# Residual tiles laid over the other branch half, late operand transposes on four banks, and the sample rows' gate and up products from the split weight pieces

## The chip, the cores and the metric

The kernel runs on one core of one Trainium2 chip. The metric is the device time of one execution in microseconds (us), lower is better. The cores' engines are called by these names: PE is TensorE, which multiplies matrices (PEld is its weight load, which stands on rows of its own), DVE is VectorE, ACT is ScalarE, POOL is GpSimd, and SP issues most of the DMA transfers.

## The reference, cut to what matters

One inference layer is computed for 1024 prompt rows and, with the same weights, for 64 sample rows (8 sequences of 8). The part that the change touches is the end of the mixing part and the convolutional feed-forward network (FFN):

```python
merged = ga * (o @ w_br_attn) + gb * (pool_out @ w_br_pool) + gm * (om @ w_br_mem)
x = x + merged @ w_out
...
h = rmsnorm(x, norm2_g)
g = h @ w_gate                       # 1024 x 2816
u = h @ w_up                         # 1024 x 2816
ext = concatenate([prefix, g])       # two rows of state ahead of each sequence
gc = conv_b + sum(conv_w[j] * ext[j:j + L] for j in range(3))
x = x + (gelu(gc) * u) @ w_down      # 2816 x 1024
```

## The kernel before, in words

All products are float32 in quality. An operand is split into a high part (a cast to the fast format, on ACT) and a low part (the difference, on DVE; helper `split`, L109 and L110), and three passes high-high, high-low and low-high are summed.

**Branch stage.** The gated branches are projected with operand tiles `ob[c][i]`, where c is the half of the tokens and i the high or low part. They live in a pool `p3`. When it closes, pool `p5` takes its place in SBUF: the residual tiles `x1_0` to `x1_7` (128 rows each), `x1s` (the 64 sample rows) and the gain `g2b` lie over the `ob` tiles, and each may be written only when the `ob` tile under it has been read for the last time.

**Output projection.** L187 multiplies by `w_out` into two PSUM banks called nat, L925 adds the residual, L926 sums squares, and L932 normalizes. SP issues in program order: the weights of `w_out` (L159), the first FFN weights (L911), `g2b` (L919), `x1s` (L948), and the eight residual tiles (L950).

**FFN operands.** The FFN's gate and up products use one level of the Strassen-Winograd scheme: seven products of quarter blocks in place of eight. The prompt's operands are B11, B21, B22 and T1 to T4; T1 to T4 are built from sums and differences (L981 to L984). `put` transposes one 128x512 piece with four PE transposes (L106) into a PSUM bank, and splits it from there. The banks of `put` come from `tpb()`, which hands out two banks, tp and av, in turn. T1 and T2 are put as soon as the tiles are normalized; T3 and T4 come last, in the loop over `late`: T3 of a pair of tiles, then T4.

**FFN products.** For each of 22 column blocks m (even m gate, odd m up; 256 columns each) `products(m)` issues seven products of 12 matmuls (L1108), each 128 weight columns by 512 wide: with weight pieces a11 (tile wA), s1 (wB), s2 (wB), a12 (wA), s3 (wC), s4 (wC), a22 (wD). Results are copied (ACT: L1127, L1130, L1133, L1145) and added (DVE: `acc`, L1124) into `gu` tiles. Between products the generator `prep(m + 1)` moves on by a step: it makes the split pieces of the next block. The convolution (L1015 to L1018) follows an even m, the product of gate and up on POOL (L1162) an odd one, and the result goes to memory (`f_d`).

**The sample rows.** `sample_ffn(m, raw)`, a generator in two halves, multiplies the 64 sample rows with the unsplit float32 weights (L1031): eight matmuls of 64 weight columns by 256 wide, which take 16 PE instructions. Its second half transposes the result (`gs`), convolves it (`conv_s`, L1022 to L1024) in an even m, and multiplies in an odd m into `fsv`. After m = 21, `fs` is the split of `fsv`.

**Down projection.** L1221 multiplies the prompt's `fh` (the split of `fr`, read back from `f_d`) with the split weights `wd`, and L1228 the sample's `fs` with the same weights.

Instructions run in order on each engine; their order across the program is decided by a scheduler when the program is built.

## Time and profile before

| | us |
|---|---|
| median of 3 runs | 1809.1 (1806.98 to 1810.25) |
| the profiled execution: its own time | 1810.49 |
| its span, first to last instruction | 1808.7 |
| PE busy in the span | 1739.5 (96%) |
| DVE, ACT, POOL busy | 899.2 (50%), 717.2 (40%), 391.7 (22%) |
| mean granted clock of TensorE | 0.987 |

A busy share close to 100% means that the engine sets the pace where that holds. Rows of a timeline give the start, the duration of the whole group, the engine, the line, the operation with its output and inputs, the shapes and the count; in brackets stands the engine's idle time before the group and what ended it. A granted clock of 1.00 is 2.4 GHz, and 0.50 is 1.2 GHz.

### The profile page before, as it was taken

To read this page: it belongs to the slowest core of one execution; us is meant where nothing else is said; L and a number is where in the kernel's file an instruction comes from. 1 tells how busy PE (TensorE), PEld (TensorE's weight loads), DVE (VectorE), ACT (ScalarE), POOL (GpSimd) and SP (SyncE) were. 2 spreads that over 40 slices of the span, in tenths; PEclk is the share of its full clock that TensorE was granted. 3 is DMA by queue.
4 is the path that set the end of the run, shared out by engine and by line. 5 is a ranking of instruction groups with operands and counts; after the bars stand their busy time and mean duration, and the time that the engine had idled before them with its cause. 6 is when DMAs were issued, how large, how long until landed. Compare 5 with 4: busy or idle time off the path is not lost.

```text
span 1808.7 us, 22927 instructions
## 1 busy us (share of the span) xinstructions
PE 1739.5 (96%) x8285; PEld 1334.1 (74%) x8285; DVE 899.2 (50%) x1543; ACT 717.2 (40%) x1396; POOL 391.7 (22%) x427
## 2 busy tenths in 40 slices
PE   7999999998999999999989899999999999999997
PEld 5887876764666777767767677777777777888876
DVE  6411134230221666677716676666666666336464
ACT  5321235331222666665413343333333334234343
POOL 1113020301101324112201344444444442000000
PEclk9999999999999999999989899999999999999999
DMA  7441251468565323154432222222222223646563
GB/s 276 139 142 66 83 183 38 135 187 266 195 230 178 96 79 117 56 193 161 145 122 88 49 72 71 71 71 71 71 71 71 71 71 135 226 145 217 197 229 109
DMA packets 137367, 234.74 MB, mean 130 GB/s; under 512 B 25679, under 2 KB 71533, under 8 KB 137253
## 3 DMA queue, kind: packets, MB, share of 16 engines
q1 hardware_dynamic: 122117, 187.16, 32.5%
q0 software_dynamic: 15136, 46.12, 6.8%
q8 instruction: 65, 1.06, 0.2%
q14 instruction: 49, 0.40, 0.1%
HBM read 182.74 MB, written 50.54 MB: 129 GB/s over the span
## 4 chain that ended last, share of the span: by engine, by line
PE 82%; issue 7%; DVE 4%; DMA 3%; ACT 2%; POOL 1%; SPq 1%; POOLq 0%; ACTq 0%; DVEq 0%
PE nat L178 17%; PE big L1108 17%; PE big L1221 10%; PE nat L1108 7%; PE nat L187 6%; PE big L178 4%; PE nat L1221 3%; PE tp L1031 3%; PE tp L106 3%; PE av L106 2%; PE av L804 2%; PE big L774 2%; PE nat L195 2%; PE av L542 1%; PE big L523 1%
## 5 line engine op out<-in xcount | busy, mean ns | idle before, releaser
L178 PE MATMUL nat<-act,hl 128*128 128x512 f32 x1344 | 357.7, 404 | 0.0
L178 PEld LDWEIGHTS nat<-act,hl 128*128 128x128 f32 x1344 | 242.1, 189 | 61.0 <-issue 14.0
L187 PE MATMUL nat<-hl,act 128*128 128x512 f32 x768 | 186.6, 401 | 10.1 <-ACT nat L926 8.3
L1221 PE MATMUL big<-wd,fh 128*128 128x512 f32 x792 | 187.4, 390 | 4.1 <-ACT big L1189 2.5
L187 PEld LDWEIGHTS nat<-hl,act 128*128 128x128 f32 x768 | 146.5, 193 | 42.3 <-ACT nat L926 8.7
L1221 PEld LDWEIGHTS big<-wd,fh 128*128 128x128 f32 x792 | 148.3, 188 | 36.3 <-ACT big L1189 3.4
L1108 PE MATMUL big<-B,wA 128*128 128x512 f32 x528 | 130.5, 395 | 0.1
L110 DVE TENSOR_TENSOR hl<-raw,hl 128x1024 fp32r<-128x1024 f32 x52 | 66.4, 1287 | 123.8 <-ACT hl L109 112.8
L110 DVE TENSOR_TENSOR wd<-wr,wd 128x1024 fp32r<-128x1024 f32 x66 | 84.5, 1282 | 74.1 <-ACT wd L109 68.2
L1108 PEld LDWEIGHTS big<-B,wA 128*128 128x128 f32 x528 | 97.4, 188 | 28.2 <-ACT gu L1133 8.3
L109 ACT CAST wd<-wr 128x1024 fp32r<-128x1024 f32 x66 | 69.3, 1052 | 83.3 <-PE tps L1228 35.3
L110 DVE TENSOR_TENSOR wB<-stm,wB 128x512 fp32r<-128x512 f32 x44 | 50.4, 1147 | 73.6 <-ACT wB L109 73.6
L568 POOL DMA_DIRECT2D gl<-ev x48 | 26.2, 546 | 277.5 <-ACT ev L567 253.2
L567 ACT COPY ev<-nat 128x512 f32<-128x512 f32 x48 | 28.1, 586 | 112.7 <-PE nat L178 106.9
L1108 PE MATMUL nat<-B,wC 128*128 128x512 f32 x264 | 69.9, 399 | 0.0
L109 ACT CAST hl<-raw 128x1024 fp32r<-128x1024 f32 x60 | 62.6, 1053 | 16.3 <-PE nat L178 8.2
L1162 POOL TENSOR_TENSOR gu<-gu,gu 128x1024 f32<-128x1024 f32 x22 | 57.0, 2591 | 52.2 <-DVE gu L1124 22.5
L1221 PE MATMUL nat<-wd,fh 128*128 128x512 f32 x264 | 67.1, 389 | 0.0
L1108 PE MATMUL big<-T,wD 128*128 128x512 f32 x264 | 66.8, 401 | 0.0
L1097 POOL TENSOR_TENSOR stm<-rf,stm 128x512 f32<-128x512 f32 x22 | 28.6, 1299 | 169.8 <-DVE wB L110 169.8
L1108 PE MATMUL big<-T,wC 128*128 128x512 f32 x264 | 64.6, 393 | 0.0
L1108 PE MATMUL nat<-T,wB 128*128 128x512 f32 x264 | 64.1, 390 | 0.0
(419 smaller groups left out, 3080.3 us busy)
## 6 DMA issues: line engine op xcount, KB each, us to landing
wr<-in_w_ffn_down SPq DMA_DIRECT2D x66, 512.0 KB
raw<-in_w_in SPq DMA_DIRECT2D x40, 512.0 KB
kr<-in_cache_k SPq DMA_DIRECT2D x64, 256.0 KB
vr<-in_cache_v SPq DMA_DIRECT2D x64, 256.0 KB
gl<-ev POOLq DMA_DIRECT2D x48, 256.0 KB, 3.0
rf<-in_w_ffn_gate SPq DMA_DIRECT2D x22, 512.0 KB
rf<-in_w_ffn_up SPq DMA_DIRECT2D x22, 512.0 KB
f_d<-gu POOLq DMA_DIRECT2D x22, 512.0 KB, 3.0
```

The costliest lines, as they stand in the source:

```text
L106: nc.tensor.transpose(out, in_, ident[:n, :n])
L109: nc.scalar.copy(hi, src)
L110: (lo_eng or nc.vector).tensor_tensor(lo, src, hi.bitcast(F32), op=ALU.subtract)
L178: nc.tensor.matmul(out, wf(k, pw)[:, n0:n0 + P], acts[c][ph][:, k, :], start=(k == ks[0] and (pw, ph) == (0, 0)), stop=(k == ks[-1] and (p ...
L187: nc.tensor.matmul(out, acts[c][ph][:, k, o:o + P], wf(k, pw), start=(k == ks[0] and (pw, ph) == (0, 0)), stop=(k == ks[-1] and (pw, ph) = ...
L195: nc.tensor.matmul(out, stack[:, k, :], wf(k, pw), start=(k == ks[0] and pw == 0), stop=(k == ks[-1] and pw == 1))
L774: nc.tensor.matmul(S[:, k0:k0 + n], Qd[:, m, part, qs], Kst[:, m, k0:k0 + n], start=(part == 0), stop=(part == 1))
L804: nc.tensor.matmul(av[:, :P], aT[:, k * P:(k + 1) * P], vn[:, k0 + k], start=(k0 + k == 0), stop=(k0 + k == i))
L1031: nc.tensor.matmul(pt[r:r + TS, 0:256], xs[:, k, 0:TS], raw[k // 4][:, k % 4], start=(k < 2), stop=(k >= 6), tile_position=(0, r))
L1108: nc.tensor.matmul(out, wt[:, pw, k], Bt[:, ph, k], start=(start and k == 0 and (pw, ph) == (0, 0)), stop=(k == 3 and (pw, ph) == (1, 0)), ...
L1162: nc.gpsimd.tensor_tensor(g[i], g[i], gts[i], op=ALU.mult)
L1221: nc.tensor.matmul(banks[i][nb], fh[:, ph, kk, i * P:(i + 1) * P], wh[:, pw, nb * 512:(nb + 1) * 512], start=(k == 0 and (pw, ph) == (0, 0 ...
```

## The change

Three edits. The first allocates the `ob` tiles with the token halves swapped, and `x1s` ahead of `x1_t`, so that the residual tiles lie over the other half's operands. The second lets the late puts take the nat banks in turn with tp and av. The third computes the sample rows from the split pieces: 16 matmuls (L1040 of the new kernel) of 128 weight columns (high and low part of the sample rows side by side, `xs`, and of their difference, `xd`) by 256 wide, in place of the 8 float32 matmuls, one step later in `prep`; the second half of the sample's work runs one block later (`late_s`), and the `gu` buffers go from six to five.

```diff
-        ob = [[p3.tile([P, KT, 512], F32R, name=f"ob{c}{i}") for i in range(2)] for c in range(2)]
+        ob = [[p3.tile([P, KT, 512], F32R, name=f"ob{c}{i}") for i in range(2)] for c in (1, 0)][::-1]
...
+        x1s = p5.tile([TS, D], F32, name="x1s")
         x1 = [p5.tile([P, D], F32, name=f"x1_{t}") for t in range(NT)]
-        x1s = p5.tile([TS, D], F32, name="x1s")
...
-        def put(Bt, xh, a):
-            pt = tpb()
+        pc = [0]
+
+        def put(Bt, xh, a, wide=False):
+            pc[0] += 1
+            pt = nat() if wide and pc[0] % 2 else tpb()
...
-                xs = ap_.tile([P, KT, P], F32, tag="hs", bufs=1, name="xs")
...
+                xs = ap_.tile([P, KT, P], F32R, tag="hs", bufs=1, name="xs")
+                to_stack(x1s, xs, KT)
+                nc.gpsimd.tensor_tensor(x1s[:, 0:512], x1s[:, 512:D], x1s[:, 0:512], op=ALU.subtract)
...
-            put(T3, xb[:, 0:512], a)
-            put(T4, xa[:, 512:D], a)
+            put(T3, xb[:, 0:512], a, True)
+            put(T4, xa[:, 512:D], a, True)
+
+        xd_ps = tpb()
+        for k in range(4):
+            tr(xd_ps[:, k * TS:(k + 1) * TS], x1s[:, k * P:(k + 1) * P])
...
+        xd = fa.tile([P, 4, P], F32R, name="xd")
+        xv = xd_ps[:, :4 * TS].rearrange("p (k t) -> p k t", k=4)
+        split(xd[:, :, 0:TS], xd[:, :, TS:P], xv)
...
-            return fa.tile([P, T], F32, tag="gu", bufs=6, name=f"gu{uid()}")
+            return fa.tile([P, T], F32, tag="gu", bufs=5, name=f"gu{uid()}")
...
-            for k in range(KT):
-                r = (k % 2) * TS
-                nc.tensor.matmul(pt[r:r + TS, 0:256], xs[:, k, 0:TS], raw[k // 4][:, k % 4], start=(k < 2), stop=(k >= 6),
-                                 tile_position=(0, r))
+            for i, (n1, n2, st2) in enumerate((("a11", "a12", xs[:, 4:8]), ("s1", "a22", xd))):
+                for k in range(KT):
+                    nc.tensor.matmul(pt[:, i * 256:(i + 1) * 256].rearrange("p (h x) -> p h x", h=2),
+                                     xs[:, k] if k < 4 else st2[:, k - 4], w[n1][:, :, k] if k < 4 else w[n2][:, :, k - 4],
+                                     start=(k == 0), stop=(k == KT - 1))
+            g4 = fa.tile([TS, 2, 2, P], F32, tag="g4", bufs=1, name=f"g4{m}")
...
-            nc.scalar.copy(gs, pt[TS:P, 0:256])
-            nc.vector.tensor_tensor(gs, pt[0:TS, 0:256], gs, op=ALU.add)
+            nc.scalar.copy(g4.rearrange("p f h x -> p (f h x)"), pt[TS:P])
+            nc.vector.tensor_tensor(g4.rearrange("p f h x -> p (f h x)"), pt[0:TS],
+                                    g4.rearrange("p f h x -> p (f h x)"), op=ALU.add)
+            nc.vector.tensor_tensor(gs.rearrange("p (f x) -> p f x", f=2), g4[:, :, 0], g4[:, :, 1], op=ALU.add)
...
             w["a12"] = piece(tA, 1, a12)
-            smp_ = sample_ffn(m, raw)
-            next(smp_)
...
-            for _ in smp_:
-                pass
+            for g_ in late_s:
+                for _ in g_:
+                    pass
+            late_s.clear()
             yield
             tD = pair("wD")
             w["a22"] = piece(tD, 0, a22)
+            yield
+            smp_ = sample_ffn(m, w)
+            next(smp_)
+            late_s.extend([smp_])
...
+        for g_ in late_s:
+            for _ in g_:
+                pass
         pt = tpb()
```

In the new kernel L1125 is what was L1108, L1040 what was L1031, L1141 what was L1124, L1241 and L1248 what were L1221 and L1228.

On PE, at the end of the output projection, the rows before run from the last `w_out` matmul to the first sample matmuls (L106 are the transposes of the puts: `x_0` to `x_7` are the residual tiles, and the output's name is the bank):

```order
L1108 MATMUL big_9802<-B_8830,wA_9741 128x512
L106 MATMUL tp_9599<-ident,x_5_8841 128x128 x4
L106 MATMUL av_9647<-ident,x_7_8843 128x128 x4
L106 MATMUL tp_9658<-ident,x_6_8842 128x128 x4
L106 MATMUL av_9665<-ident,x_7_8843 128x128 x4
L106 MATMUL tp_9674<-ident,x_1_8837 128x128 x4
L106 MATMUL av_9681<-ident,x_0_8836 128x128 x4
L106 MATMUL tp_9688<-ident,x_3_8839 128x128 x4
L106 MATMUL av_9695<-ident,x_2_8838 128x128 x4
L106 MATMUL tp_9702<-ident,x_5_8841 128x128 x4
L106 MATMUL av_9709<-ident,x_4_8840 128x128 x4
L106 MATMUL tp_9716<-ident,x_7_8843 128x128 x4
```

The same place in the new kernel:

```order
L106 MATMUL nat_9704<-ident,x_5_8842 128x128 x4
L1125 MATMUL big_9799<-B_8830,wA_9751 128x512 x2
L106 MATMUL av_9649<-ident,x_7_8844 128x128 x4
L106 MATMUL tp_9660<-ident,x_6_8843 128x128 x4
L106 MATMUL nat_9718<-ident,x_7_8844 128x128 x4
L106 MATMUL av_9667<-ident,x_7_8844 128x128 x4
L106 MATMUL tp_9683<-ident,x_0_8837 128x128 x4
L106 MATMUL av_9697<-ident,x_2_8839 128x128 x4
L106 MATMUL tp_9711<-ident,x_4_8841 128x128 x4
L106 MATMUL av_9725<-ident,x_6_8843 128x128 x4
L106 MATMUL tp_9732<-ident,x1s 128x64 x4
L1040 MATMUL av_9777<-wA_9751,xs 128x256 x8
```

The T3 puts of x_1, x_3 and x_5 now stand in nat banks ahead of x_7's first put or among the first FFN product; that of x_7 is in nat too. The four T4 puts still alternate between tp and av, and a put of the sample's difference (`x1s`, 64 columns each) follows them.

On PE, in one block of the FFN well inside the loop, before (wA, wB, wC, wD are the weight pieces, B and T the prompt's operands, `rf` the unsplit weights):

```order
L1108 MATMUL big_10436<-T_9673,wD_10429 128x512 x12
L1108 MATMUL big_10589<-B_8830,wA_10457 128x512 x12
L1108 MATMUL nat_10590<-T_9389,wB_10473 128x512 x12
L1108 MATMUL big_10589<-T_9390,wB_10473 128x512 x12
L1031 MATMUL tp_10663<-rf_10453,xs 64x256 x4
L1031 MATMUL tp_10663<-rf_10455,xs 64x256
L1108 MATMUL big_10589<-B_8831,wA_10457 128x512 x12
L1031 MATMUL tp_10663<-rf_10455,xs 64x256 x3
L1108 MATMUL nat_10590<-B_8832,wC_10535 128x512 x2
```

And in the new kernel, from the transposes ahead of a block's seventh product to the fourth product of the next block:

```order
L106 MATMUL tp_10427<-ident,gs_10302 128x64 x2
L1040 MATMUL av_10447<-wA_10339,xs 128x256 x3
L1125 MATMUL big_10318<-T_9675,wD_10281 128x512 x12
L1040 MATMUL av_10447<-wA_10339,xs 128x256 x5
L1040 MATMUL av_10447<-wB_10355,xs 128x256 x4
L1040 MATMUL av_10447<-wD_10444,xd 128x256 x4
L1125 MATMUL big_10473<-B_8830,wA_10339 128x512 x12
L1125 MATMUL nat_10474<-T_9391,wB_10355 128x512 x12
L1125 MATMUL big_10473<-T_9392,wB_10355 128x512 x12
```

The sample's matmuls moved from around the fourth product to the end of the block before; three stand ahead of the seventh product and 13 behind it, the last four of them with wD of the next block.

On PE, at the end of the FFN's first part, before (`gc` is the prompt's conv state, `fh` the prompt's down operand, `fs` the sample's):

```order
L1108 MATMUL big_13121<-T_9673,wD_13106 128x512 x12
L106 MATMUL tp_13220<-ident,gc 44x128
L1228 MATMUL av_13246<-wd_13253,fs 128x512 x2
L1228 MATMUL av_13246<-wd_13280,fs 128x512 x2
L1228 MATMUL tps<-wd_13253,fs 128x512 x2
L1228 MATMUL tps<-wd_13280,fs 128x512 x2
L1228 MATMUL av_13246<-wd_13310,fs 128x512 x2
L1228 MATMUL tps<-wd_13310,fs 128x512 x2
L1221 MATMUL big_13242<-wd_13253,fh_13237 128x512
```

In the new kernel, from the same product:

```order
L1125 MATMUL big_13347<-T_9675,wD_13310 128x512 x12
L106 MATMUL tp_13446<-ident,gs_13331 128x64 x2
L106 MATMUL av_13450<-ident,gc 44x128
L1241 MATMUL big_13472<-wd_13483,fh_13467 128x512
L1241 MATMUL big_13473<-wd_13483,fh_13467 128x512
L1241 MATMUL nat_13474<-wd_13483,fh_13467 128x512
L1241 MATMUL nat_13475<-wd_13483,fh_13467 128x512
L1248 MATMUL av_13476<-wd_13483,fs 128x512 x2
L1248 MATMUL tps<-wd_13483,fs 128x512 x2
L1241 MATMUL big_13472<-wd_13483,fh_13467 128x512 x5
```

The last sample transposes now come behind the last product, and of the 13 sample matmuls that stood ahead of the prompt's sixth down matmul, four remain there.

## Rows read from the trace of the kernel before

**Rows 1.** The page's line of busy time, share of the span and instructions of each engine.

```profile
PE 1739.5 (96%) x8285; PEld 1334.1 (74%) x8285; DVE 899.2 (50%) x1543; ACT 717.2 (40%) x1396; POOL 391.7 (22%) x427
```

**Rows 2.** Stretches of the span: from and to, length, busy time and instructions of PE, PEld, DVE, ACT and POOL, granted clock, DMA share, GB/s.

```profile
800.00:804.00 4.00, 4.00 (x11) 3.04 (x10) 3.25 (x5) 1.11 (x2) 0.00 (x0) 0.50 0.27 88
900.00:920.00 20.00, 11.28 (x40) 8.49 (x39) 5.84 (x8) 2.31 (x6) 0.00 (x0) 0.76 0.91 309
1024.00:1028.00 4.00, 2.38 (x11) 1.63 (x10) 2.11 (x4) 1.76 (x3) 1.83 (x2) 0.50 0.00 0
1040.00:1044.00 4.00, 4.00 (x20) 2.67 (x17) 4.00 (x4) 2.91 (x9) 3.84 (x3) 0.99 0.41 129
1100.00:1500.00 400.00, 400.00 (x1824) 302.09 (x1824) 247.75 (x292) 159.81 (x302) 159.54 (x141) 1.00 0.21 71
1536.00:1540.00 4.00, 2.41 (x11) 1.63 (x10) 4.00 (x4) 1.30 (x2) 2.12 (x4) 1.00 0.94 364
```

**Rows 3.** The timeline of SP, DVE and PE at the start of the output projection.

```profile
903.11 0.34 SPq L919 DMA_DIRECT2D g2b<-in_norm_g  x1
...
913.19 1.41 DVE L925 TENSOR_TENSOR x1s<-x1s,nat 64x512 f32<-64x512 f32 x2 [8.72 <-DMA x1s<-in_x_sample]
...
915.54 2.07 PE L187 MATMUL nat<-hl,act 128*128 128x512 f32 x4 [8.32 <-ACT nat L926]
```

**Rows 4.** The timeline of PE at the late puts.

```profile
1028.01 1.09 PE L106 MATMUL av<-ident,x 128*128 128x128 f32 x4 [0.64 <-DVE T L110]
...
1035.75 1.09 PE L106 MATMUL av<-ident,x 128*128 128x128 f32 x4 [0.64 <-POOL stm L1093]
1036.76 3.56 PE L1031 MATMUL tp<-rf,xs 128*64 128x256 f32 x16
1040.25 0.96 PE L1108 MATMUL nat<-T,wB 128*128 128x512 f32 x3
```

**Rows 5.** The timeline of DVE in one turn of the late puts.

```profile
1029.75 0.69 DVE L110 TENSOR_TENSOR T<-av,T 128x512 fp32r<-128x512 f32 x1 [1.03 <-ACT T L109]
```

**Rows 6.** The timeline of PE in the FFN: the first products of m = 1 (1060.61) and of m = 21 (1513.17), between them one block (from 1128.72), and last the row behind the seventh product of m = 21.

```profile
1060.61 1.75 PE L1108 MATMUL big<-B,wA 128*128 128x512 f32 x7
...
1128.72 2.88 PE L1108 MATMUL big<-B,wA 128*128 128x512 f32 x12
1131.44 2.88 PE L1108 MATMUL nat<-T,wB 128*128 128x512 f32 x12
...
1136.98 1.51 PE L1031 MATMUL tp<-rf,xs 128*64 128x256 f32 x10
1138.42 3.03 PE L1108 MATMUL big<-B,wA 128*128 128x512 f32 x12
1141.38 1.08 PE L1031 MATMUL tp<-rf,xs 128*64 128x256 f32 x6
1142.38 0.74 PE L1108 MATMUL nat<-B,wC 128*128 128x512 f32 x2
...
1513.17 2.88 PE L1108 MATMUL big<-B,wA 128*128 128x512 f32 x12
...
1532.62 0.27 PE L106 MATMUL tp<-ident,gc 128*44 128x128 f32 x1
```

**Rows 7.** The timeline of PE in the attention stage: narrow matmuls between wide ones, each followed by the row behind it.

```profile
628.89 0.41 PE L774 MATMUL big<-Kst,Qd 128*128 128x256 f32 x2
629.13 1.09 PE L178 MATMUL nat<-act,hl 128*128 128x512 f32 x4
...
706.93 1.06 PE L804 MATMUL av<-vn,aT 128*128 128x128 f32 x8
707.83 0.49 PE L106 MATMUL tp<-ident,E 128*128 128x128 f32 x3
```

**Rows 8.** Weight loads by line: durations in ns (least, median, most), first and last start, forms.

```profile
L804 PEld LDWEIGHTS av<-vn,aT x288: 186/192/192, 590.9 to 757.5; 128*128 128x128 f32 x144
L1108 PEld LDWEIGHTS big<-B,wA x528: 186/188/190, 1013.8 to 1524.6; 128*128 128x128 f32 x176
```

**Rows 9.** The timeline of POOL and DVE in an odd block, where the sample's convolution ran beside POOL's product of gate and up.

```profile
1171.50 2.83 POOL L1162 TENSOR_TENSOR gu<-gu,gu 128x1024 f32<-128x1024 f32 x1 [2.24 <-DVE gu L1124]
...
1171.38 0.69 DVE L110 TENSOR_TENSOR wD<-rf,wD 128x512 fp32r<-128x512 f32 x1
1171.99 2.61 DVE L1022 TENSOR_SCALAR fsv<-es,cwb 128x64 f32<-128x64 f32 x2
1174.52 0.47 DVE L1023 SCALAR_TENSOR_TENSOR fsv<-es,cwb,fsv 128x64 f32<-128x64 f32 x2
```

**Rows 10.** The timeline of ACT, DVE and PE between the FFN's last block and the down projection.

```profile
1520.21 1.37 ACT L109 CAST fs<-fsv 128x1408 fp32r<-128x1408 f32 x1
...
1534.60 0.83 ACT L109 CAST fh<-fr 128x768 fp32r<-128x768 f32 x1
...
1521.62 1.63 DVE L110 TENSOR_TENSOR fs<-fsv,fs 128x1408 fp32r<-128x1408 f32 x1 [2.93 <-ACT fs L109]
...
1537.50 2.69 DVE L110 TENSOR_TENSOR fh<-fr,fh 128x768 fp32r<-128x768 f32 x3
...
1538.50 2.56 PE L1221 MATMUL big<-wd,fh 128*128 128x512 f32 x10 [1.59 <-DVE fh L110]
```

**Rows 11.** The timeline of PE in the branch stage, behind an idle stretch.

```profile
798.67 5.46 PE L178 MATMUL nat<-ob,hl 128*128 128x512 f32 x12 [3.25 <-DVE ht L871]
```

More of the change, by code (lines that the diff above doesn't have):

```diff
@@ L958, in hybrid_step @@
                 norm2(x1s, TS, NT)
-                xs = ap_.tile([P, KT, P], F32, tag="hs", bufs=1, name="xs")
-                pt = tpb()
-                for k in range(KT):
-                    tr(pt[:, k * TS:(k + 1) * TS], x1s[:, k * P:(k + 1) * P])
-                nc.scalar.copy(xs[:, :, 0:TS], pt.rearrange("p (k t) -> p k t", k=KT))
+                xs = ap_.tile([P, KT, P], F32R, tag="hs", bufs=1, name="xs")
+                to_stack(x1s, xs, KT)
+                nc.gpsimd.tensor_tensor(x1s[:, 0:512], x1s[:, 512:D], x1s[:, 0:512], op=ALU.subtract)
             for i, t in enumerate((0, 2, 1, 3, 4, 6, 5, 7) if nb else range(NT)):
@@ L1024, in conv_s, with sample_ffn @@
             nc.vector.scalar_tensor_tensor(out, e[:, :, 2:2 + DS], cwb[:, f, 2:3], out, op0=ALU.mult, op1=ALU.add)
-        def sample_ffn(m, raw):
+        def sample_ffn(m, w):
             j, c0 = m // 2, (m // 2) * 256
             pt = tpb()
-            for k in range(KT):
-                r = (k % 2) * TS
-                nc.tensor.matmul(pt[r:r + TS, 0:256], xs[:, k, 0:TS], raw[k // 4][:, k % 4], start=(k < 2), stop=(k >= 6),
-                                 tile_position=(0, r))
+            for i, (n1, n2, st2) in enumerate((("a11", "a12", xs[:, 4:8]), ("s1", "a22", xd))):
[4 more added lines that the diff above has]
+            g4 = fa.tile([TS, 2, 2, P], F32, tag="g4", bufs=1, name=f"g4{m}")
             gs = fa.tile([TS, 256], F32, tag="gs", bufs=2, name=f"gs{m}")
-            nc.scalar.copy(gs, pt[TS:P, 0:256])
-            nc.vector.tensor_tensor(gs, pt[0:TS, 0:256], gs, op=ALU.add)
+            nc.scalar.copy(g4.rearrange("p f h x -> p (f h x)"), pt[TS:P])
+            nc.vector.tensor_tensor(g4.rearrange("p f h x -> p (f h x)"), pt[0:TS],
+                                    g4.rearrange("p f h x -> p (f h x)"), op=ALU.add)
+            nc.vector.tensor_tensor(gs.rearrange("p (f x) -> p f x", f=2), g4[:, :, 0], g4[:, :, 1], op=ALU.add)
             yield
@@ L1056, in sample_ffn @@
                 nc.scalar.activation(a, a, AF.Gelu_apprx_tanh)
-        wts = {}
+        wts, late_s = {}, []
         def prep(m):
```

## The prediction, made before the kernel ran

> **What bounds the kernel now.** The page's busy shares come first: PE 96% of the span, the next one, DVE, 50% [rows 1]. Then the stretches. In the FFN loop PE is busy without a gap, 400.00 us of 400, at full granted clock, while DVE has 247.75 us (62%), ACT 159.81 and POOL 159.54 [rows 2]. There a microsecond of PE work is a microsecond of time, and ACT or DVE work is free as long as it comes in time. Then I read timelines where PE waits. Three of those places are touched. At the start of the output projection PE idles 8.32 us behind the residual data, while DMA moves 309 GB/s [rows 2, 3]. At the late puts PE stops 0.64 us ahead of each av put, and two puts take (1035.75 − 1028.01) / 3 = 2.58 us [rows 4]. Between the FFN and the down projection it idles 1.59 us for `fh` [rows 10].
>
> **Edit 1, halves swapped: 0.** Before, the `x1_t` that lie over the c = 1 operands wait for the last c = 1 matmuls. But SP issues in order, and `g2b`, which stands ahead of `x1s` and all `x1_t`, goes out at 903.11, behind the weights of the output projection, when the branch matmuls are already over. The tiles under `x1_t` coming free one step earlier lets nothing start earlier while that order stands. From there the time is transfer: `x1s` is first used at 913.19, and PE goes on at 915.54 [rows 3]. I take 0. If SP were not the holder, one step of 24 matmuls, 24 × 0.227 = 5.4 us, would be the most; I bound the gain by 5.
>
> **Edit 2, late puts: −3.8.** Before, all eight T3 and T4 puts run in the two-bank turn, and the sample and the second product start behind them, at 1036.76 and 1040.25 [rows 4]. In the new order three T3 puts (of x_1, x_3, x_5) move up to the first product, where PE had idle time waiting for x_7's norm. Behind x_7's norm, T3 of x_7 has a bank of its own; four T4 puts and the small `xd` put keep the turn of 2.58. So the turn holds five puts in place of eight: 3 × 1.29 = 3.9 us less. Against it, the three moved puts bring three subtractions on DVE of 0.69 us [rows 5] ahead of x_7's norm, which is on the path. All three would cost 2.1; DVE's order takes the pair differences of x_5 and x_7's residual add a few places earlier, and from laying the rows in the new order I take +0.8. Net −3.1. The sample of m = 0 takes 3.49 us there (1036.76 to 1040.25), and PE's clock is back at 0.99 only in the stretch from 1040 [rows 2, 4]. The new 16 matmuls lie partly in the cold stretch: half of the way from 3.49 to the 2.0 of a warm one, −0.75. Together −3.8, with bounds of 0 (DVE gives all of it back, cold price kept) and −6 (no DVE cost, the clock back sooner).
>
> **Edit 3, the sample in the loop: −13.6.** A sample takes 1.44 us (1136.98 to 1138.42) and 1.00 (1141.38 to 1142.38) directly. The product between them takes 2.96 where an undisturbed one takes 2.72 (1128.72 to 1131.44), and the seams at other products come to another 0.1: 2.8 us [rows 6]. As a check, 20 blocks from 1060.61 to 1513.17 take 22.63 us each, and m = 21, which holds no sample, takes 19.45 to 1532.62; the difference is 3.18, with about 0.25 of it the small transposes [rows 6]. The new sample is 16 matmuls of 128 weight columns by 256. The nearest rows: two matmuls 256 wide with 128 weight columns take 629.13 − 628.89 = 0.24, so 0.12 each, and eight matmuls with 128-column loads take 707.83 − 706.93 = 0.90, so 0.113 each [rows 7]; a long run keeps that pace too. Half of a 512-wide one (0.227) is 0.114. With 0.12, 16 cost 1.92, with 0.2 for two seams 2.12. The saving is 0.68 per block, and 20 blocks give −13.6. Bounds: if the seams cost as much as now (0.55), 0.33 per block, −6.6; with 0.115 and almost no seam, 0.9, −18. The old matmuls were mixed into products of another kind of operand, the new ones have the same, so I stand nearer to the upper half than to the lower.
>
> The same block has more work on ACT and DVE (a copy of 512 columns for 256, two additions for one, about 0.7 us of DVE per block), which lies beside PE's 100%. What was late in no row but can be now is wD: the last four sample matmuls need the a22 piece of the next block right behind the seventh product, and its buffer comes free with the sixth. PE has ahead of it the transposes, three narrow matmuls, the product and nine more: 0.3 + 0.36 + 2.72 + 1.08 = 4.4 us. DVE does in that time its `acc` (0.69), in an even block six short convolution instructions at 0.24 (two L1023 take 0.47), and the subtraction of wD (0.69): 2.8 [rows 9]. So there are 1.6 us to spare, and I cost it at 0. The cover is thin: before, two L1022 beside POOL's L1162 took 2.61 where 0.47 is usual [rows 9]. In the new order the convolution falls in even blocks, and L1162 in odd ones. If they met again, DVE would need 2.8 + 2.1 = 4.9 and PE would wait 0.5. Five `gu` buffers in place of six: the POOL product that frees the fifth is done some 7 us ahead of need, no cost. Splitting `xs` and `xd` costs a few DVE and ACT instructions once, beside the output projection.
>
> **The end of the loop: +5.0.** Before, `fs` was split at 1520.21 and 1521.62, far ahead, and 13 sample down matmuls filled PE's time until `fh`'s low part was there; 1.59 us stayed idle [rows 10]. Now the last sample's second half stands behind product 7, so the cast of `fs` (1.37, ACT) and its subtraction (1.63, DVE) come there, right ahead of `fh`'s (the first of three in 2.69). One subtraction of `wd` has moved behind `fh`, so `fh` is ready about when it was. But nine of the 13 filling matmuls are now behind that point: 9 × 0.227 = 2.0 us more idle, with 0.3 of transposes 2.3. That makes an idle of about 3.6 us. In this trace the granted clock stayed at 1.00 around an idle of 1.59 [rows 2], while behind one of 3.25 us 12 matmuls took 5.46 us in place of 2.72 [rows 11], +2.7. I take both, +5.0. Bounds 2.3 (the clock holds) and 6 (`fh` comes later too).
>
> **Sum.** −3.8 − 13.6 + 5.0 = −12.4. Against the profiled execution's own 1810.49 that is 1798.1; that execution stands 1.4 above the median, and from the median, 1809.1, I get 1796.7.
>
> **A rule that speaks against the change.** The Trainium skill, page "TensorE: Matmul & The Clock Gate", section "Part 3: Packing small matmuls — row/col tiling", says that a weight load overlaps with matmuls in flight only when its row group differs. Here all narrow matmuls use the same rows, so by it each pays its load: the first rival below. The trace disagrees: 12 matmuls of one row group take 2.72 us while each has a load of its own of 0.188 [rows 6, 8], so loads do lie under matmuls; how far they do under 256-wide ones is told by [rows 7] alone.
>
> **Rivals.**
> 1. Weight loads pace the narrow matmuls. If a load (0.188) can't begin before the one ahead has ended, 16 cost 3.0 + 0.2, 0.4 more than before: +8, sum +9, 1818. If it lies beside nothing, 0.308 each, 2.3 more: +46, sum +48, 1857. It decides from 0.158 per matmul on (16 × 0.158 + 0.2 = 2.73, where the sum is 0). Against it are the eight in 0.90 with loads of 0.192 each [rows 7, 8]. Chance 3%.
> 2. wD comes late behind product 7, and PE waits for it. At 0.5 us in every block, it gives back 10: 1807, about no change. From 12.4 / 20 = 0.62 per block it makes the kernel slower; at 1.0 in every block, 1817. For it: the sample's step is the last of `prep`, on three engines in turn, and the slow L1022. Against: 1.6 us to spare by rows. Chance 5% for slower, 12% for a partial one of about 0.4 per block (+8, 1805).
> 3. The puts bring nothing and the end costs most (0 and +6): −13.6 + 6 = −7.6, 1801.5. For it: the five T4 and `xd` puts still alternate between two banks, and x_7's norm is later. Chance 15%.
> 4. The swap works after all, −5: 1791.7. For it: the next thing on SP may go earlier by the scheduler. Against: 309 GB/s, the transfer itself. Chance 5%.
>
> **How the numbers follow.** My forecast has 60%, 1796.7, by its own bounds 1790 to 1803. The range for 8 in 10 takes in rivals 3 and 4 and most of the partial rival 2: 1788 to 1805. A change under 0.2% (3.6 us) can't be told from none. Faster: 60 + 15 + 5 and half of the partial rival 2, 86%. Same: the other half and a bit, 7%. Slower: rivals 1 and 2 with errors not thought of, 7%.
>
> **What would show it.** In the new profile, 16 L1040 in 1.9 to 2.0 us with no wait ahead of the last four, and blocks of 21.95 us in place of 22.63 (wrong: an idle ahead of L1040 by DVE or ACT at wD, or narrow matmuls at 0.16 or more). The first L1040 starts at about 1033.7 (1036.76 − 3.1); at 1036.8 the late puts have brought nothing. The 8.32 us stop at the output projection unchanged (wrong: under 7). PE idle of 3 to 4 us ahead of the first long run of L1241, and a granted clock near 0.5 behind it. If the sum is wrong, the likeliest step is the end or the seams.

## The result and the profile after

The changed kernel takes 1794.18 us, median of 4 runs (1792.74 to 1797.69), for 1808.88 of the kernel before. The ratio is 0.9922 with an interval of 0.9904 to 0.9941: about 14 us faster, forecast 12.4.

The page's line of busy time, which answers to [rows 1]:

```profile
PE 1723.9 (96%) x8289; PEld 1350.5 (75%) x8289; DVE 891.2 (50%) x1567; ACT 722.8 (40%) x1397; POOL 394.1 (22%) x428
```

PE has about as many instructions as before and 15.6 us less busy time. Where the time went is seen best by cutting the execution at rows that all kernels have. Each number is the difference of the starts of two rows: the first L187 matmul of the output projection; the first FFN product; the first PE row behind the late puts; the first product of the second block; that of the last block; the transposes of `gc` behind the last product; the end of the span.

| stretch, us | before | changed |
|---|---|---|
| to the output projection | 901.61 | 898.46 |
| output projection | 112.37 | 111.93 |
| first FFN product to the end of the late puts | 22.78 | 18.91 |
| rest of the first block | 23.85 | 23.98 |
| 20 blocks | 452.56 | 438.03 |
| last block | 19.45 | 19.96 |
| down projection and end | 276.08 | 279.73 |

The first line is not the change. In the profiles of thirteen kernels with the same instructions up to there, the output projection starts anywhere from 897.04 to 902.37, so 3 us of the 17.7 between these two profiles are scatter. The five lines from the first FFN product on add up to −14.1, as the ratio has it.

The timeline of PE at the late puts, changed kernel, which answers to [rows 4]:

```profile
1010.39 0.71 PE L1125 MATMUL big<-B,wA 128*128 128x512 f32 x2
...
1018.51 1.11 PE L106 MATMUL av<-ident,x 128*128 128x128 f32 x4 [2.90 <-DVE x L932]
...
1022.60 1.06 PE L106 MATMUL tp<-ident,x 128*128 128x128 f32 x4
1024.21 1.11 PE L106 MATMUL av<-ident,x 128*128 128x128 f32 x4 [0.55 <-DVE T L110]
1025.12 1.06 PE L106 MATMUL tp<-ident,x 128*128 128x128 f32 x4
1026.82 1.09 PE L106 MATMUL av<-ident,x 128*128 128x128 f32 x4 [0.64 <-POOL stm L1097]
1027.83 0.69 PE L106 MATMUL tp<-ident,x1s 64*128 64x64 f32 x4
1029.30 2.07 PE L1040 MATMUL av<-wA,xs 128*128 128x256 f32 x8 [0.78 <-DVE T L110]
1031.17 1.05 PE L1125 MATMUL nat<-T,wB 128*128 128x512 f32 x2
```

The turn of tp and av is still there, but it is shorter by three puts. The two rows of the kernel before that answer to the first two, the first FFN product and x_7's first put:

```profile
1013.98 2.43 PE L1108 MATMUL big<-B,wA 128*128 128x512 f32 x10
...
1022.15 0.63 PE L106 MATMUL av<-ident,x 128*128 128x128 f32 x4 [1.91 <-DVE x L932]
```

x_7's put comes as far behind the first product as before (8.12 us, 8.17 before), though one moved put (1010.03) now stands between the last `w_out` matmul and that product. The gain lies behind x_7's put. The timeline of PE in one odd block, which answers to [rows 6]; the sample is in L1040:

```profile
1070.29 0.62 PE L1040 MATMUL av<-wA,xs 128*128 128x256 f32 x3
1070.75 2.91 PE L1125 MATMUL big<-T,wD 128*128 128x512 f32 x12
1073.50 0.76 PE L1040 MATMUL av<-wA,xs 128*128 128x256 f32 x5
1074.09 0.64 PE L1040 MATMUL av<-wB,xs 128*128 128x256 f32 x4
1074.57 0.64 PE L1040 MATMUL av<-wD,xd 128*128 128x256 f32 x4
1075.05 2.91 PE L1125 MATMUL big<-B,wA 128*128 128x512 f32 x12
```

Four narrow matmuls take 0.48 us (1074.09 to 1074.57). The sample's four rows take 2.01 us, 0.1 of it at the seams with the wide product, and that product takes 2.75 for an undisturbed 2.72: 2.04 us for a sample that took 2.8. The block goes from 22.63 to 21.90. PE still has no idle in the loop.

The timeline of PE behind the last product, which answers to [rows 10], and the stretches around it:

```profile
1511.27 0.29 PE L106 MATMUL av<-ident,gc 128*44 128x128 f32 x1
1514.80 0.73 PE L1241 MATMUL big<-wd,fh 128*128 128x512 f32 x2 [3.23 <-ACT fh L109]
1515.37 0.63 PE L1241 MATMUL nat<-wd,fh 128*128 128x512 f32 x2
1516.18 1.09 PE L1248 MATMUL av<-wd,fs 128*128 128x512 f32 x2 [0.18 <-DVE fs L110]
1517.07 1.06 PE L1248 MATMUL tps<-wd,fs 128*128 128x512 f32 x2
1517.92 3.33 PE L1241 MATMUL big<-wd,fh 128*128 128x512 f32 x10
1521.09 1.09 PE L1241 MATMUL nat<-wd,fh 128*128 128x512 f32 x4
```

```profile
1512.00:1516.00 4.00, 1.20 (x4) 0.67 (x4) 2.57 (x3) 3.36 (x4) 3.98 (x5) 1.00 1.08 400
1516.00:1520.00 4.00, 3.82 (x10) 3.04 (x11) 3.87 (x5) 1.16 (x2) 0.25 (x1) 0.57 0.94 355
1520.00:1524.00 4.00, 4.00 (x19) 3.29 (x18) 0.70 (x1) 1.05 (x1) 0.00 (x0) 1.00 0.81 247
```

PE idles 3.23 us ahead of the first prompt matmul of the down projection, and 0.18 more ahead of the first sample one, where it idled 1.59 in all, and the granted clock of the next stretch is 0.57: the 14 matmuls from 1516.18 to 1521.09 take 4.91 us, where 14 at 0.227 take 3.18.

### The profile page after: what moved, and what is told of

It is laid out like the page before. It is cut to its first block, busy times and chain, and to the rows that moved or that the text cites. A ratio compares the mean times of both kernels' runs of the same rounds, so it can differ in the third digit from the quotient of the medians.

```text
span 1791.0 us, 23026 instructions
## 1 busy us (share of the span) xinstructions
PE 1723.9 (96%) x8289; PEld 1350.5 (75%) x8289; DVE 891.2 (50%) x1567; ACT 722.8 (40%) x1397; POOL 394.1 (22%) x428
## 4 chain that ended last, share of the span: by engine, by line
PE 84%; DVE 5%; DMA 4%; issue 3%; ACT 2%; SPq 1%; POOL 1%; POOLq 0%; ACTq 0%; DVEq 0%
PE big L1125 17%; PE nat L178 16%; PE big L1241 10%; PE nat L187 8%; PE nat L1125 7%; PE big L178 4%; PE tp L106 3%; PE nat L1241 3%; PE av L1040 3%; PE av L804 2%; PE big L774 2%; PE nat L195 2%; PE av L106 1%; DMA raw<-in_w_in 1%; PE av L542 1%
## 5 line engine op out<-in xcount | busy, mean ns | idle before, releaser
L187 PE MATMUL nat<-hl,act 128*128 128x512 f32 x768 | 185.7, 399 | 9.6 <-ACT nat L926 7.9
L1241 PE MATMUL big<-wd,fh 128*128 128x512 f32 x792 | 188.3, 391 | 5.8 <-ACT fh L109 3.2
L1241 PEld LDWEIGHTS big<-wd,fh 128*128 128x128 f32 x792 | 149.2, 189 | 37.9 <-ACT fh L109 3.4
L187 PEld LDWEIGHTS nat<-hl,act 128*128 128x128 f32 x768 | 145.4, 191 | 41.4 <-ACT nat L926 8.3
L1125 PE MATMUL big<-B,wA 128*128 128x512 f32 x528 | 131.1, 396 | 0.0
L1125 PEld LDWEIGHTS big<-B,wA 128*128 128x128 f32 x528 | 95.9, 188 | 24.3 <-ACT gu L1150 6.3
L1125 PE MATMUL nat<-B,wC 128*128 128x512 f32 x264 | 70.5, 389 | 0.0
L1108 POOL TENSOR_TENSOR stm<-rf,stm 128x512 f32<-128x512 f32 x22 | 28.7, 1303 | 189.2 <-DVE wB L110 189.2
L1241 PE MATMUL nat<-wd,fh 128*128 128x512 f32 x264 | 67.2, 389 | 0.0
L1125 PE MATMUL big<-T,wC 128*128 128x512 f32 x264 | 66.4, 400 | 0.0
L1125 PE MATMUL nat<-T,wB 128*128 128x512 f32 x264 | 65.2, 395 | 0.0
L1125 PE MATMUL big<-T,wD 128*128 128x512 f32 x264 | 64.1, 391 | 0.0
L1125 PE MATMUL big<-T,wB 128*128 128x512 f32 x264 | 63.4, 389 | 0.0
```

Source lines behind the costliest of these rows:

```text
L187: nc.tensor.matmul(out, acts[c][ph][:, k, o:o + P], wf(k, pw), start=(k == ks[0] and (pw, ph) == (0, 0)), stop=(k == ks[-1] and (pw, ph) = ...
L1108: nc.gpsimd.tensor_tensor(s4, a12, s2, op=ALU.subtract)
L1125: nc.tensor.matmul(out, wt[:, pw, k], Bt[:, ph, k], start=(start and k == 0 and (pw, ph) == (0, 0)), stop=(k == 3 and (pw, ph) == (1, 0)), ...
L1241: nc.tensor.matmul(banks[i][nb], fh[:, ph, kk, i * P:(i + 1) * P], wh[:, pw, nb * 512:(nb + 1) * 512], start=(k == 0 and (pw, ph) == (0, 0 ...
```

## The experiments

**Each edit alone on the kernel before.** The diffs are those of the three edits, one at a time.

First edit. 

> The kernel before with the first edit alone (halves swapped, x1s first). Theory (the transfers behind g2b hold the start of the output projection, not the tiles' release): no change, within 0.2%, and the stop behind the residual data stays near 8.3 us. Rival (the 3.15 us by which the new profile is already ahead when the output projection starts, and the 0.4 us shorter stop, come from the swap): 3 to 4 us faster.

Measured: ratio 1.0003 (0.9994 to 1.0012). The stop behind the residual data is 7.62 us in its profile; in the other profiles with the same loads it lies between 6.61 and 8.43, so the 7.62 says nothing. No gain of the swap can be measured here, and the head start of the changed kernel's profile isn't its.

Second edit. 

> The kernel before with the second edit alone (late puts also on the nat banks). Theory: about 3.9 us faster, since the first sample matmul comes that much earlier after the first FFN matmul, and nothing behind it gives it back. Rival (the moved subtractions delay the norm of x_7 by as much, and the gain in the new kernel came from edits together): no change.

Measured: ratio 0.9997 (0.9986 to 1.0008). The theory fell as it was put: the puts alone bring no gain that can be measured. Its profile shows a gain and two losses. From the first FFN product to the end of the late puts it takes 19.56 for 22.78, and then 25.09 for 23.85 to the second block: 2.0 us less in all, which the interval (up to 2.5 us faster) doesn't exclude. The timeline of PE there:

```profile
1014.21 1.17 PE L1111 MATMUL big<-B,wA 128*128 128x512 f32 x4
...
1024.17 1.09 PE L106 MATMUL av<-ident,x 128*128 128x128 f32 x4 [3.64 <-DVE x L932]
...
1033.77 3.06 PE L1034 MATMUL tp<-rf,xs 128*64 128x256 f32 x16
1036.76 2.34 PE L1111 MATMUL nat<-T,wB 128*128 128x512 f32 x9
1040.48 0.34 PE L106 MATMUL av<-ident,gs 64*128 64x64 f32 x2 [1.38 <-DVE gs L1038]
```

The first loss is the rival's: x_7's first put comes 9.96 us behind the first product, 1.8 later than before, because DVE now subtracts for three moved puts ahead of x_7's norm (T<-nat at 1015.93, 1019.27 and 1021.39 in its timeline). From there to the first sample matmul it takes 9.60 for 14.61. The second loss: the second half of the first sample stands in the middle of the second product, as the scheduler placed it, and PE waits 1.38 us there for DVE's addition of `gs`. In the changed kernel that half runs a block later (the third edit), so the two edits look tied; an experiment below takes that wait away alone.

Third edit. 

> The kernel before with the third edit alone (sample from split pieces, five gu buffers). Theory: -14.5 us in the loop (20 blocks of 21.90 for 22.63) and +4.2 at its end (0.25 in the last block and 3.9 behind it): about 10.4 us faster. Rival (the loss at the end is not from this edit, but from the ready time of the prompt's data read back): 14.5 us faster.

Measured: ratio 0.9953 (0.9937 to 0.9969), 8.5 us faster with 5.6 to 11.4. The theory's 10.4 lies in it, the rival's 14.5 does not. Its profile has the same 438.03 us for 20 blocks, 280.90 for the last stretch, and 23.77 (for 22.78) to the end of the late puts, since the `xd` put belongs to this edit: x_7's first put comes 7.56 us behind the first product, and from there to the first sample matmul it takes 16.21.

**The puts with the first sample's second half held back.** On the kernel before with the second edit:

```diff
-        wts = {}
+        wts, held = {}, []
...
-            for _ in smp_:
-                pass
+            if m == 0:
+                held.append(smp_)
+            else:
+                for g_ in held + [smp_]:
+                    for _ in g_:
+                        pass
+                held.clear()
```

> The kernel before with the second edit alone, and the second half of the first block's sample held back by one block, as the third edit does it for all. Theory (the puts alone gave back 1.2 us because the transposes of the first sample then wait 1.38 us for DVE in the middle of the second product, at the low clock): that wait is gone, the stretch from the late puts' end to the second block takes 23.8 us in place of 25.1, and the time is 3.2 us below before's. Rival (it is given back somewhere else): the stretch shortens and the time stays within 1 us of before.

Measured: ratio 0.9969 (0.9957 to 0.9981), 5.6 us faster. The theory had 3.2, just out of the interval (3.4 to 7.8). The stretch behind the late puts takes 22.31 us where the theory had 23.8, because the clock came back earlier as well. The stretch from 1028 in the profile of this kernel, and then from 1028, 1032 and 1036 in that of the puts alone:

```profile
1028.00:1032.00 4.00, 3.13 (x17) 2.41 (x16) 2.53 (x5) 2.24 (x4) 1.38 (x2) 0.76 0.14 1
```

```profile
1028.00:1032.00 4.00, 3.59 (x17) 2.75 (x15) 2.08 (x5) 2.24 (x4) 0.93 (x2) 0.50 0.21 2
1032.00:1036.00 4.00, 3.69 (x18) 2.00 (x18) 2.49 (x4) 2.80 (x6) 3.08 (x3) 0.50 0.96 11
1036.00:1040.00 4.00, 3.10 (x17) 1.91 (x13) 4.00 (x4) 2.96 (x6) 3.60 (x3) 0.99 0.58 35
```

PE's instructions up to there are the same in both, in the same order, and still the clock rose some 6 us apart. So part of the difference of these two profiles is not the wait, and as the profiled execution of this kernel is one of its slowest (1807.27 us, the median of 9 is 1804.44), its profile can't say how much of the 5.6 us is. What is shown: with the second half held back, the puts gain 3.4 to 7.8 us on the kernel before, and without it no gain can be measured. This 5.6 and the third edit's 8.5 add up to 14.1, the whole of the measured gain; each is uncertain by 2 to 3 us, so the agreement to the tenth is luck.

**The end of the loop.** `fs` is finished and split behind the second product of the last block:

```diff
+        def last_s():
+            yield
+            for g_ in late_s:
+                for _ in g_:
+                    pass
+            late_s.clear()
+            yield
+            fs = ap_.tile([P, NF, P], F32R, tag="act", bufs=4, name="fs")
+            split(fs[:, :, 0:TS], fs[:, :, TS:P], fsv)
+            fs_box.append(fs)
+
+        fs_box = []
...
-            nxt = prep(m + 1) if m + 1 < 2 * NG else iter(())
+            nxt = prep(m + 1) if m + 1 < 2 * NG else last_s()
...
-        for g_ in late_s:
-            for _ in g_:
-                pass
...
-        fs = ap_.tile([P, NF, P], F32R, tag="act", bufs=4, name="fs")
-        split(fs[:, :, 0:TS], fs[:, :, TS:P], fsv)
+        fs = fs_box[0]
```

> The changed kernel, with the last sample's second half and the split of fs moved up into the last block (behind its second product), so that 11 to 13 sample down matmuls stand again between the last product and the prompt's sixth down matmul. Theory (the loss at the end is the order of fs's split): the 3.9 us come back, 4 us faster than the changed kernel, PE idle there about 1.6 us and the clock at 1.00. Rival (the wait is for the prompt's data from memory whatever PE does): the idle stays over 3 us and nothing is gained.

Measured: 1791.16 us, ratio to before 0.9904 (0.989 to 0.9917), 3.0 below the changed kernel's median. The two intervals overlap, but the last stretch takes 276.01 us in this profile, for 279.73 to 280.90 in the kernels with the third edit and without this one. PE's timeline:

```profile
1511.62 1.17 PE L1256 MATMUL tps<-wd,fs 128*128 128x512 f32 x4
...
1515.51 0.39 PE L1256 MATMUL av<-wd,fs 128*128 128x512 f32 x1
1517.41 2.57 PE L1249 MATMUL big<-wd,fh 128*128 128x512 f32 x10 [1.51 <-DVE fh L110]
```

```profile
1516.00:1520.00 4.00, 2.59 (x11) 2.17 (x12) 3.09 (x4) 0.44 (x1) 1.02 (x2) 1.00 0.99 300
```

The fillers are back, the idle is 1.51, and the clock stays at 1.00. The other profiles say the same. From the transposes of `gc` to a row late in the down projection (the first prompt matmul behind a wait of 1.81 us) it takes 204.56 to 204.68 us in the seven profiles in which `fs` is split early, with PE idle 1.23 to 1.59 and the clock at 1.00, and 207.75 to 208.82 in the six in which it is split late, with a first idle of 3.23 to 3.26 and the clock down to 0.50 behind it. What is left to the end takes 71.4 to 71.5 or 73.1 us, whatever the edits, so the last stretches scatter by 1.6 us on their own. The loss was the order of `fs`'s split, not the data read back.

**How much spare time wD has.** The two groups of the sample's matmuls are issued in the other order, so that wD is used sooner:

```diff
-            for i, (n1, n2, st2) in enumerate((("a11", "a12", xs[:, 4:8]), ("s1", "a22", xd))):
+            for i, (n1, n2, st2) in enumerate((("s1", "a22", xd), ("a11", "a12", xs[:, 4:8]))):
+                i = 1 - i
```

> The changed kernel with the sample's two groups in the other order, so that the four matmuls with wD stand 0.96 us earlier, one matmul behind the seventh product. If the spare time were the 1.6 us of the prediction in every block: no change. By the new profile wD's subtraction takes 2.90 us in an odd block, beside POOL's product, and ends 0.59 us before it is used, so about 0.4 us of wait in each of 10 odd blocks: 4 us slower, and none in even blocks.

Measured: 1798.17 us, 4.0 above the changed kernel, ratio to before 0.9945 (0.9931 to 0.9958). This interval overlaps that of the changed kernel, but the 20 blocks take 443.46 for 438.03, 5.4 us more, or 0.54 per odd block. Two rows of wD in PE's timeline, of an odd and of an even block:

```profile
1071.30 0.74 PE L1041 MATMUL av<-wD,xd 128*128 128x256 f32 x4 [0.28 <-DVE wD L110]
...
1093.44 0.64 PE L1041 MATMUL av<-wD,xd 128*128 128x256 f32 x4
```

The wait is there in odd blocks alone. The reason is in the changed kernel's timelines of POOL and DVE, of an odd block (from 1070) and then an even one, with the PE row in which the even block's wD is first used:

```profile
1071.05 2.39 POOL L1179 TENSOR_TENSOR gu<-gu,gu 128x1024 f32<-128x1024 f32 x1 [0.75 <-DVE gu L1141]
...
1070.29 0.68 DVE L1141 TENSOR_TENSOR gu<-gu,nat 128x512 f32<-128x512 f32 x1
1071.08 2.90 DVE L110 TENSOR_TENSOR wD<-rf,wD 128x512 fp32r<-128x512 f32 x1
...
1092.85 0.54 DVE L1031 TENSOR_SCALAR fsv<-es,cwb 128x64 f32<-128x64 f32 x2
...
1094.09 0.68 DVE L110 TENSOR_TENSOR wD<-rf,wD 128x512 fp32r<-128x512 f32 x1
...
1096.61 0.64 PE L1040 MATMUL av<-wD,xd 128*128 128x256 f32 x4
```

wD's subtraction starts 0.03 us behind POOL's product and takes 2.90 where it takes 0.68 alone. It ends at 1073.98, 0.59 ahead of its first use at 1074.57; in the even block 1.84 ahead of 1096.61. All ten odd blocks have 2.90 or 2.91 there, and the even ones 0.68 or 0.69.

**What paces a narrow matmul.** Each sample matmul is cut into two of 128 columns:

```diff
-                    nc.tensor.matmul(pt[:, i * 256:(i + 1) * 256].rearrange("p (h x) -> p h x", h=2),
-                                     xs[:, k] if k < 4 else st2[:, k - 4], w[n1][:, :, k] if k < 4 else w[n2][:, :, k - 4],
-                                     start=(k == 0), stop=(k == KT - 1))
+                    for h in range(2):
+                        nc.tensor.matmul(pt[:, i * 256 + h * P:i * 256 + (h + 1) * P],
+                                         xs[:, k] if k < 4 else st2[:, k - 4],
+                                         w[n1][:, h, k] if k < 4 else w[n2][:, h, k - 4],
+                                         start=(k == 0), stop=(k == KT - 1), skip_group_check=True)
```

This kernel and the next one serve for timing alone; what they leave out of the sample's sums is told in the next expectation.

> The changed kernel with each of the 16 sample matmuls cut in two of 128 columns, so the same columns stream and twice as many weights are loaded. Theory (the stream sets the pace, loads lie under it): 32 matmuls at 0.06 us, no change. Rival (a load of 128 weight columns paces a narrow matmul, at the 0.113 us of the eight in 0.90 of the attention stage): 3.6 us for 1.92 per block, 21 blocks, 35 us slower.

Measured: 1835.78 us, 41.6 above the changed kernel, ratio to before 1.0144 (1.0127 to 1.0162). The theory fell: the 20 blocks take 471.76 for 438.03, 33.7 more, as the rival had it. The first block, where the sample and the second product run at the low clock, makes 6.5 of the rest (30.50 for 23.98 behind the late puts). Then the same with 64 weight columns, as a change of the half-wide kernel:

```diff
-                        nc.tensor.matmul(pt[:, i * 256 + h * P:i * 256 + (h + 1) * P],
-                                         xs[:, k] if k < 4 else st2[:, k - 4],
+                        nc.tensor.matmul(pt[0:TS, i * 256 + h * P:i * 256 + (h + 1) * P],
+                                         xs[:, k, 0:TS] if k < 4 else st2[:, k - 4, 0:TS],
...
-            nc.scalar.copy(g4.rearrange("p f h x -> p (f h x)"), pt[TS:P])
+            nc.scalar.copy(g4.rearrange("p f h x -> p (f h x)"), pt[0:TS])
```

> The changed kernel with each sample matmul cut in two of 128 columns, as in the experiment on half-wide matmuls, and with the high part of the sample rows alone as weights, 64 columns in place of 128 (the low part is left out, and in both kernels the accumulations of the halves disturb one another, so the sample's outputs are not the reference's; the instructions are the same in number). Theory (weight loads pace a narrow matmul): with loads of half the columns eight take clearly less than 0.89 us, down to 0.5. Rival (a 128-column stream itself takes 0.11 us): eight take 0.89 us as before.

Of each kernel one row of PE's timeline with the row behind it, and a row of its weight loads (shortest, median and longest in ns):

```profile
1084.78 1.06 PE L1041 MATMUL av<-wB,xs 128*128 128x128 f32 x8
1085.67 1.06 PE L1041 MATMUL av<-wD,xd 128*128 128x128 f32 x8
...
L1041 PEld LDWEIGHTS av<-wB,xs x176: 192/192/333, 1036.0 to 1533.8; 128*128 128x128 f32 x176
```

```profile
1080.18 0.64 PE L1041 MATMUL av<-wB,xs 128*64 128x128 f32 x8
1080.66 0.64 PE L1041 MATMUL av<-wD,xd 128*64 128x128 f32 x8
...
L1041 PEld LDWEIGHTS av<-wB,xs x176: 134/135/227, 1032.3 to 1498.7; 128*64 128x64 f32 x176
```

Eight half-wide matmuls take 0.89 us with 128 weight columns, 0.111 each, and 0.48 us with 64, 0.060 each. The stream is the same, the load differs, and the 20 blocks go back from 471.76 to 440.32 us in this kernel's one run. So a load of 128 columns allows one matmul per 0.111 us, and the 0.120 of a 256-wide one lies just above it. With 64 columns the pace is half of that 0.120, as the stream alone would have it, so what the smaller load would allow is not shown, only that it is no slower. The Trainium skill, page "TensorE: Matmul & The Clock Gate", section "LDWEIGHTS (loading the stationary operand)", gives a load P / 1.2 ns for P columns; by it an estimate for the two loads is 107 and 53 ns. The 0.111 us is near the first, and the 0.060 doesn't speak against the second.

**Other ways to gain.** The load of `g2b` behind the residual tiles:

```diff
-        nc.sync.dma_start(g2b, bc(norm2_g[0], P))
...
                     nc.sync.dma_start(x1[t], x_prompt[t * P:(t + 1) * P])
+                nc.sync.dma_start(g2b, bc(norm2_g[0], P))
```

> The changed kernel, with g2b's load issued behind the residual tiles in place of ahead of them. Theory (the start of the output projection waits for transfers): 0.5 MB less stands ahead of x1s, which is 1.7 us at 300 GB/s, and one issue of 0.4 us; the stop of 7.9 us gets 1.5 to 2.2 us shorter, and the time falls by as much. Rival (SP is held by the weight load ahead of g2b, and the transfers under way then end at the same time anyway): no change.

Measured: 1794.24 us (1790.39 to 1794.34), ratio to before 0.9916 (0.9902 to 0.9929), the median of the changed kernel. The stop did get shorter, 5.52 us here and 5.86 in the last kernel below, under the 6.61 to 8.43 of all profiles with the old order, and yet the time didn't fall by what these runs can tell. Whether 2 us are given back later or lie within the scatter stays open.

More of the late puts on nat, with the end's repair in it:

```diff
-            pt = nat() if wide and pc[0] % 2 else tpb()
+            pt = nat() if wide else tpb()
...
-            put(T3, xb[:, 0:512], a, True)
-            put(T4, xa[:, 512:D], a, True)
+            put(T3, xb[:, 0:512], a, a < 3)
+            put(T4, xa[:, 512:D], a, a % 2 == 1)
...
-        xd_ps = tpb()
+        xd_ps = nat()
```

> The changed kernel with the earlier split of fs (the experiment on the end), and the late puts dealt to the four banks so that three T4-like puts stay in the turn of two banks in place of five (T3 of x_1, x_3, x_5, T4 of x_2 and x_6 and the sample's difference go to nat). Theory (the turn of 2.58 us per two puts is what is left there): two puts fewer in the turn, 2 us less between the first FFN product and the first sample matmul (18.9 in the changed kernel), about 1789. Rival (the norm of x_7 is delayed by one more subtraction ahead of it and the puts then wait for DVE): 18.9 stays, as in the experiment on the end alone.

Measured: 1792.16 us, ratio to before 0.9901 (0.9887 to 0.9915). The stretch to the end of the late puts takes 18.40 for 18.92 of the end's repair alone: a quarter of the 2 us. Theory and rival both hold in part: from x_7's first put to the first sample matmul it takes 9.58 for 10.78, but that put comes 8.82 us behind the first product for 8.14. Its timeline has the puts waiting for DVE's work on the tiles in place of the banks:

```profile
1023.46 1.12 PE L106 MATMUL av<-ident,x 128*128 128x128 f32 x4 [2.59 <-DVE x L932]
...
1026.67 1.09 PE L106 MATMUL av<-ident,x 128*128 128x128 f32 x4 [1.24 <-DVE x L981]
```

> The kernel of the experiment on the four banks, with g2b's load behind the residual tiles too. Theory: what its parts gave, added: 0 to 2 us faster than without the later g2b load; about 1788. Rival (the parts hide one another): the same as the experiment on the end alone, 1791.

Measured: 1791.75 us, ratio 0.9898 (0.9883 to 0.9912). The last three versions with the end's repair can't be told from one another. All lie 2 to 3 us below the changed kernel's median, with intervals of the ratio that overlap its interval; the plainest, the repair alone, is the one to keep.

## Why the prediction was right, point by point

The time lies in the range, and the three terms come in the main from the mechanisms that the runs show, with the sizes off by less than 1 us each: by rows −3.7, −14.5 and +4.2, for −3.8, −13.6 and +5.0.

- **The swap, 0.** Right, by the experiment alone: 1.0003. That transfers ahead of `x1s` hold the start fits the shorter stop with a later `g2b`; that SP's order is what keeps an earlier release from helping was argued, not tested.
- **The late puts, −3.8.** The sum is right, two of its terms are not. The turn lost three puts: from x_7's first put to the first sample matmul it took 14.61 us (1022.15 to 1036.76) and takes 10.79 (1018.51 to 1029.30), −3.82 for the −3.9 worked out. x_7's norm was to come 0.8 later by the moved subtractions; counted from the first FFN product, its put comes no later (8.12 for 8.17). The delay is real, though: it is 1.8 with the second edit alone (9.96), and 0.6 when the second edit is added to the third (8.12 for 7.56). The rest of the first block was to give 0.75 and took 0.13 more. These two misses cancelled, so that the sum came out at −3.7 is luck. What the prediction did not see is that this gain hangs on the third edit: alone, the puts run into the wait of the first sample's transposes.
- **The sample, −13.6.** 20 blocks gave −14.5. The price of 0.12 per matmul held to the last digit (four in 0.48); the seams cost 0.1, not 0.2, and that is the miss. The bound with 0.115 was out of reach: 0.120 is twice the 0.060 of the half-wide ones with small loads, so it is what 256 columns take, while the loads alone would have allowed 0.111.
- **wD's spare time, 1.6 us.** Wrong for every second block. The prediction looked at what the short convolution does beside POOL's product, and saw it move to the even blocks. It did not ask which instruction comes to stand in its place in the odd ones. It was wD's own subtraction, which went to 2.90 and left 0.59. No time was lost by it, but the cover is thin: used 0.96 us earlier, wD costs 0.54 in each odd block. The even blocks have 1.84 to spare, near the 1.6.
- **The end, +5.0.** The last block and the last stretch together take 4.2 more. The idle is 3.41 in two pieces for the 3.6 worked out; the larger one stands ahead of the first prompt matmul, which waits for ACT's cast of `fh` behind that of `fs`, and not ahead of the long run. The cold clock cost 1.7 (4.91 for 3.18), not 2.7. The price had been taken from a row of 12 matmuls at the low clock throughout; here the stretch from 1520 is at 1.00 again.
- **The rivals.** The weight loads don't pace the 256-wide matmuls, but by 0.009 us. The prediction gave that 3%, on the row of eight in 0.90, whose 0.113 was the load's pace itself; nothing that the prediction read of the trace of before told whether it was the load's or the stream's.

## What to carry to other kernels

When work is moved off a contended place, look for what comes to stand there in its stead, on every engine that shares something with it. Keep a filler for each hand-over between stages: what was split early by habit was, here, what kept PE and its clock going, and one edit of a few lines gave back about 3 us. And price edits together where one moves what the other runs into: the second edit brought no gain that could be measured alone, and with the third 4.6 us by the rows (18.91 and 23.98 for 23.77 and 23.75) or 5.6 by the times (14.1 less 8.5, uncertain by some 4).

## What the runs showed of the hardware

- A float32 subtraction of DVE with both inputs in SBUF took 2.90 us for 0.68 when it began 0.03 us behind a POOL product of two SBUF tiles of 2.39 us (2.90 or 2.91 in all ten odd blocks of the loop). The Trainium skill, page "SBUF — State Buffer", section "SBUF: two separate sides", says that a DVE instruction with two SBUF inputs and a POOL instruction that reads SBUF take turns by a lock held for a whole instruction, and the row agrees: 2.36 us of waiting for POOL's end and the 0.68 of its own make 3.04, near the 2.90.
- A weight load of 128 columns allowed one matmul per 0.111 us, one of 64 columns per 0.060 or faster, though each load's own row shows 0.192 and 0.135. The duration of a load's row is not its pace.
- The granted clock came back some 6 us apart in two kernels whose PE instructions are the same up to the earlier of the two rises (0.76 and 0.50 in the stretch from 1028), so a single profile is poor evidence for a difference at a cold stretch.
